# A hybrid layer on one core: seven-product pairs in every wide chunk, the plain pair first in gate/up, and four smaller moves

## The chip, the cores and the metric

One core of a Trainium2 chip runs the whole layer. The metric is device time in microseconds, from three timed runs; one further execution was profiled, and all rows come from that one. The engines are TensorE (PE, its weight loads PEld), VectorE (DVE), ScalarE (ACT), GpSimd (POOL) and SyncE (SP), which issues the loads.

## The reference, cut to what matters

256 tokens, model width 2048, all float32:

```
x = x + 0.5 * swiglu(rmsnorm(x, ffn1_norm), w_gate, w_up, w_down)       # width 5632
proj = rmsnorm(x, mix_norm) @ w_in                                      # ten parts
ro = retention(rope(rq), rope(rk), rv), normed, * silu(rg)              # 8 heads
ao = attention over the 64 best keys of each query, by an index score    # 8 heads, 2 kv
x = x + concat([ro, ao]) @ w_out                                        # 2048 x 2048
x = x + 0.5 * swiglu(rmsnorm(x, ffn2_norm), w_gate, w_up, w_down)
out = rmsnorm(x, final_norm)
```

## The kernel before, in words

**Numbers.** Every operand is split into hi and lo, both float32r: hi is ScalarE's rounding copy (line 269 for weights), lo is VectorE's difference (line 275). A product is three matmuls: hi·hi, left hi with right lo, left lo with right hi. A matmul has 512 columns.

**Wide chunks.** The gate/up, down and w_out products go in chunks of 1024 columns (`wide`, line 174): 256 tokens (two tiles, t = 0, 1) by two column halves (c = 0, 1). The contraction goes by pairs, two blocks of 128 each, 1 MB of weights a pair. A plain pair ("C") makes 8 block products of three matmuls, 24, straight into the four sums. A pair of seven products ("S", Strassen's way, Winograd's form) makes 7, so 21, in the banks of `S_BLOCKS` (line 168). For S, VectorE subtracts weight blocks from each other (line 261, four operations of 512 columns a pair), and the left side is cut into sums by `blocks_of` (line 292). A chunk's plan names its pairs: `PLAIN` has no S, `UP` is SCSCSCCC, `DOWN` has four S and then C's. The first gate/up chunk of each FFN and both w_out chunks are PLAIN; the other 20 gate/up chunks are UP; all down chunks are DOWN.

**Banks.** Eight PSUM banks. M2, M3, M4, M8 (`MAP_B`) hold the four sums 11, 12, 21, 22; M1, M5, M6, M7 hold products that several sums need (and under `MAP_A` the sums of a PLAIN chunk). After the last S pair of a chunk (`s_end`), `sums_of` (line 439) reads M1, M5, M6, M7 into the tiles u, in three steps: one copy and one addition; then the transposes of the hidden tiles of the chunk before (`turn`, line 525, in M1 and M6); then three additions. One step before the chunk's end, `ups` (line 507) adds M3 and M8 to u; at its end `hidden` (line 512) adds M2 and M4, applies silu on ScalarE and multiplies. In down and w_out, `grow` (line 457) does the like onto x.

**Order.** All is written out by hand. The list `pieces` holds the steps: a plain pair is two pieces (the first for c = 1, banks M3 and M8, the second for c = 0, M2 and M4; 12 matmuls each), an S pair four (6, 6, 6 and 3 matmuls). A load has 2048 columns, in three buffers; hi and lo have five buffers each. The loop at line 1035 goes through the pieces: in step i it runs what `after` put there, then issues the split of piece i + 4 (i + 2 for the first 11 pieces), then the matmuls of piece i:

```
        while n_split < min(n, i + ahead):
            split(n_split)
            n_split += 1
        run_step(i)
        if n_split < min(n, i + ahead + 1):
            split(n_split)
```

Each engine works its queue in that order. FFN1's chunks have numbers 0 to 5 (part 0, then down) and 6 to 10 (part 1, then down); a chunk's hidden tiles are turned in the next chunk, the left two of a chunk one for S and one plain where `DOWN` asks for it.

**Elsewhere.** `first_x`, `x_for` and `s_of_x` (lines 321 to 357) make the left sides of x from its transpose, in FFN1's first chunk as the loads come in, later from PE transposes (`turn_x`, line 359). `tables` (line 612) makes the rotation tables on VectorE, one to three operations a step, from the start of part 1 of FFN1. `first_squares` (line 655) and `rstd_tok` (line 409) give the norm. `finish` (line 571) takes squares of the last quarter of x, the norm, the products and four transfers of the output; `gain_first` (line 1025) multiplies the first half of x by the final gain, eight steps before the end.

Of the kernel before, what the change touches and what calls it, by code (L numbers as in the profile page):

```python
# [28 lines left out]
PLAIN = "CCCCCCCC"  # L29
UP = "SCSCSCCC"  # L30
# [19 lines left out]
def layer(ctx: ExitStack, tc: tile.TileContext, a: dict, out: bass.AP):  # L50
# [32 lines left out]
    MAP_A = {"11": "M7", "12": "M1", "21": "M6", "22": "M5"}  # L83
    MAP_B = {"11": "M2", "12": "M3", "21": "M4", "22": "M8"}
    turn = [0, 0]

    def pair():
        turn[0] += 1
        return [[bank["M1"], bank["M5"]], [bank["M6"], bank["M7"]]][turn[0] % 2]

    def small():
        turn[1] += 1
        return [bank["M2"], bank["M3"], bank["M4"], bank["M8"]][turn[1] % 4]
# [12 lines left out]

    now = [0]
# [66 lines left out]
    def wide(src, plan, left, cmap, x0=False):  # L174

        start = len(pieces)
        seen, last = {}, {}
        s_end = None

        def mm(i, off, a, m):  # L180

            for n, (u, v) in enumerate(((0, 0), (0, 1), (1, 0))):
                st = m not in seen
                seen[m] = 1
                e = [i, off, a, m, u, v, st, False]
                last[m] = e
                pieces[i]["mms"].append(e)

        for p, kind in enumerate(plan):
# [14 lines left out]
            if kind == "C":  # L204
                for c in (1, 0):
                    for k in range(2):
                        off = 1024 * (1 - c) + 512 * k
                        j = max(j for j, (o, n) in enumerate(tiles) if o <= off)
                        for t in range(2):
                            mm(i + j, off - tiles[j][0], (t, k), cmap[f"{t + 1}{c + 1}"])  # L210
            else:
                for k, off, a, m in S_BLOCKS:
                    mm(i + k, off, a, m)
                s_end = len(pieces)
        for e in last.values():
            e[7] = True
        return start, s_end, len(pieces) - 1, len(pieces)

    def run_mms(p, hi, lo):
        for _, off, a, m, u, v, st, sp in p["mms"]:  # L220
            TE.matmul(bank[m], lhsT=p["left"](p["pair"], a)[u], rhs=(hi, lo)[v][:, off:off + 512], start=st, stop=sp)  # L221
# [60 lines left out]
    def split_x(c, norm, xT, t=None):  # L282

        if t is None:
            t = new(one, [P, 2, 512], F32R, f"xg{c}")
# [22 lines left out]

    def s_block(pair, a):
# [99 lines left out]
    def rstd_tok(norm):  # L409
        v = new(tmp, [P, 2], F32, "sum_v", 1)  # L410
        s, k = squares[norm]
        V.tensor_reduce(v, s[:, :, :k[0]], axis=AX.X, op=OP.add)
        V.tensor_scalar(v, v, 1.0 / D, EPS, op0=OP.mult, op1=OP.add)
        r_tok[norm] = new(one, [P, 2], F32, f"r_tok{norm}")
        rsqrt(r_tok[norm], v, 2)
# [41 lines left out]
    def grow(d, scale, at, cmap, norm, done=None):  # L457
# [9 lines left out]
        def ready(c):  # L467
            for t in range(2):
                add_x(t, d, c, bank[cmap[f"{t + 1}{c + 1}"]], scale)

        if s_end is not None:
            after(s_end, early)
        after(half, lambda: ready(1))
# [9 lines left out]
    marks = {}  # L483

    def ffn(which, norm, next_norm, last):
        wgu, wd = a[f"wgu{which}"], [a[f"wd{which}{j}"] for j in range(2)]
        c = 0
        for part, n in enumerate(PARTS):
            hs = {}
            marks[which, part] = len(pieces)  # L490
            for cc in range(n):
                cmap = MAP_A if c == 0 else MAP_B
# [4 lines left out]
                if s_end is not None:  # L497
                    after(s_end, lambda u=u: sums_of(u))

                def full(b, u=u, cmap=cmap):  # L500

                    if b in u:
                        tt(u[b], u[b], bank[cmap[b]])
                        return u[b]
                    return bank[cmap[b]]

                def ups(u=u, full=full):
                    for b in ("12", "22"):
                        if b in u:
                            full(b)  # L510

                def hidden(u=u, full=full, cc=cc, part=part, hs=hs, cmap=cmap):
                    ht, sil = [], []
                    for t in range(2):
                        g = full(f"{t + 1}1")
                        s = u[f"{t + 1}1"] if u else new(tmp, [P, W], F32, "s")
                        S.activation(s, g, AF.Silu, scale=r_tok[norm][:, t:t + 1])  # L517
                        sil.append(s)
                    for t in range(2):
                        b = f"{t + 1}2"  # L520
                        ht.append(u[b] if u else new(tmp, [P, W], F32, "e", 3))
                        V.scalar_tensor_tensor(ht[t], u[b] if u else bank[cmap[b]], r_tok[norm][:, t:t + 1], sil[t],  # L522
                                               op0=OP.mult, op1=OP.mult)

                    def turn(m, q):
# [5 lines left out]
                        if DOWN[part][k] == "S":  # L531
                            f = half_k("b")
                            S.activation(f, v, AF.Copy)
                            hs[k] = blocks_of(f, big(F32R, (P, 4, 2, P)), big(F32R, (P, 3, 2, P)))
                        else:
                            h = big(F32R, (P, 2, 512))
                            S.activation(h[:, :, :T], v, AF.Copy)
                            V.tensor_tensor(h[:, :, T:], v, h[:, :, :T].bitcast(F32), op=OP.subtract)
                            hs[k] = h
# [8 lines left out]
            for d in range(2):  # L548
                at = wide(wd[part][d], DOWN[part], left_of(hs), MAP_B)
                start, s_end, half, end = at  # L550
                final = last and part == 1 and d == 1
                if part == 1 and d == 0:
                    after(end, lambda: act_table(AF.Sqrt))
                grow(d, 0.5, at, MAP_B, next_norm if part == 1 and not final else None)
                if final:
                    after(end, finish)
                elif part == 1 and not last:
                    if d == 0:
                        turns = list(range(4))
                    else:  # L560
                        for i, m in enumerate(("M1", "M5", "M6", "M7")):
                            after(s_end + 2 + i, lambda i=i, m=m: turn_x(i, next_norm, m))
                        turn_rest(end, next_norm)
        return end

    def turn_rest(end, norm):

        for s, c, m in ((0, 6, "M3"), (0, 7, "M8"), (1, 4, "M2"), (1, 5, "M4")):
            after(end + s, lambda c=c, m=m: turn_x(c, norm, m))

    def finish():

        for c in (1, 0):
            for t in range(2):
                square_x(3, t, halves(2 + c).start, 512)
        rstd_tok(3)
        for t in range(2):
            r = r_tok[3][:, t:t + 1]
            xs = [x[t][:, halves(c, 1024)] for c in range(2)]
            S.activation(xs[0], xs[0], AF.Copy, scale=r)  # L580
            V.scalar_tensor_tensor(xs[1], xs[1], r, last_gain[1], op0=OP.mult, op1=OP.mult)
            for c in range(2):
                nc.sync.dma_start(out[t][:, halves(c, 1024)], xs[c])
# [20 lines left out]
    V.memset(ones, 1.0)  # L604
    act_table(AF.Copy)
# [6 lines left out]
    def tables(at_sin):  # L612
# [13 lines left out]
        yield 1  # L626
        V.tensor_scalar(n, n, MAGIC, None, op0=OP.add)
        yield 1
        V.tensor_scalar(n, n, MAGIC, None, op0=OP.subtract)
        for c in (C1, C2, C3):  # L630
            yield 1
# [3 lines left out]
        yield 1  # L635

        V.tensor_scalar(n, ang, 1.0 / C_TWO_PI, MAGIC, op0=OP.mult, op1=OP.add)
        yield 1
        V.tensor_scalar(n, n, MAGIC, None, op0=OP.subtract)
        for c in (C1, C2, C3):  # L640
            yield 1
            V.scalar_tensor_tensor(ang, n, -c, ang, op0=OP.mult, op1=OP.add)
        yield 1
        V.tensor_scalar(ang, ang, PI_DOWN, -PI_DOWN, op0=OP.min, op1=OP.max)
        yield 1
# [208 lines left out]
    def attend(pair):  # L854
# [17 lines left out]
        m = big(F32R, (P, 2, 512))  # L872
# [260 lines left out]
```

## Time and profile before

| what | value |
|---|---|
| three timed runs | 1887.64, 1888.31, 1888.44 us; median 1888.31 |
| the profiled execution | 1887.65 us |
| its span, first to last instruction | 1885.8 us |
| TensorE, VectorE, ScalarE busy | 98%, 86%, 56% |
| matmuls | 8624 |
| weights and other reads | 355.76 MB, 190 GB/s over the span |
| chain that ended last, by engine | PE 93%, DVE 5%, ACT 1%, issue 1% |
| granted TensorE clock, mean | 0.997 |

The chain is followed back from the last instruction: at each step to what released it. A row of the timeline gives start, duration, engine, line, operation, what is written and read, how many alike were merged, and in brackets the idle time before it with what ended it. Matmuls overlap in it: each has its full passage as duration, and the next starts before it ends.

### The profile page before, as it was taken

How to read it: one execution, taken by the hardware profiler on the slowest of the kernel's cores; microseconds unless marked ns; L12 is line 12 of the kernel's file. 1: busy time of each engine (PE TensorE's matmuls, PEld its weight loads, DVE VectorE, ACT ScalarE, POOL GpSimd, SP SyncE). 2: the span in 40 equal slices, each digit the busy share in tenths (PEclk: the TensorE clock that was granted, in tenths of full speed). 3: DMA queues.
4: the chain of work that ended last, by engine and by line, in shares of the span. 5: the costliest groups of instructions: out<-in, count | busy, mean ns of one | idle time of the engine just before them, and what ended most of it. 6: DMA issues, size and time to landing. Idle time of an engine off the chain costs nothing.

```text
span 1885.8 us, 22691 instructions
## 1 busy us (share of the span) xinstructions
PE 1856.2 (98%) x8624; PEld 1527.1 (81%) x8624; DVE 1625.8 (86%) x2076; ACT 1064.9 (56%) x1348; POOL 5.3 (0%) x14
## 2 busy tenths in 40 slices
PE   8999999999999999999999999999999999999997
PEld 6788888887888887988888888788888888888886
DVE  7899998889999997789865756799999889999997
ACT  7555655544555555656544555555555455555554
POOL 0000000000000000000000000000000000000000
PEclk9999999999999999999999999999999999999998
DMA  8544555545555454545534444545555555455454
GB/s 323 191 178 180 199 201 221 192 170 178 194 206 203 172 208 156 187 164 211 179 134 173 168 174 178 198 181 191 209 203 180 199 201 200 180 191 210 180 198 159
DMA packets 51309, 359.33 MB, mean 191 GB/s; under 512 B 5856, under 2 KB 5856, under 8 KB 8704
## 3 DMA queue, kind: packets, MB, share of 16 engines
q1 hardware_dynamic: 50400, 355.62, 51.6%
q8 instruction: 67, 1.10, 0.2%
q10 hardware_dynamic: 432, 1.08, 0.2%
q0 software_dynamic: 368, 1.19, 0.2%
q14 instruction: 42, 0.34, 0.1%
HBM read 355.76 MB, written 2.10 MB: 190 GB/s over the span
## 4 chain that ended last, share of the span: by engine, by line
PE 93%; DVE 5%; ACT 1%; issue 1%; DMA 0%; DVEq 0%; ACTq 0%
PE M L221 75%; PE M L145 8%; PE M L147 4%; DVE lo L275 2%; PE M L529 1%; PE M L163 1%; PE M L164 1%; PE M L162 1%; DVE raw L261 1%; DVE x L434 1%; ACT hi L269 1%; PE M L790 0%; DVE e L437 0%; PE M L838 0%; PE M L144 0%
## 5 line engine op out<-in xcount | busy, mean ns | idle before, releaser
L269 ACT ACTIVATE hi<-raw 128x1024 fp32r<-128x1024 f32 (+2 forms) x853 | 843.9, 1008 | 578.8 <-DVE raw L261 356.3
L275 DVE TENSOR_TENSOR lo<-raw,hi 128x1024 fp32r<-128x1024 f32 (+2 forms) x853 | 974.5, 1160 | 152.7 <-ACT hi L269 137.7
L221 PE MATMUL M<-hi,xg 128*128 128x512 f32 x2240 | 738.3, 396 | 1.4 <-DVE e L437 1.4
L221 PE MATMUL M<-hi,mid 128*128 128x512 f32 x1696 | 531.1, 392 | 8.2 <-ACT hi L269 7.8
L221 PEld LDWEIGHTS M<-hi,xg 128*128 128x128 f32 x2240 | 422.6, 189 | 99.5 <-DVE e L437 1.9
L221 PE MATMUL M<-lo,xg 128*128 128x512 f32 x1120 | 444.4, 397 | 2.3 <-DVE lo L275 2.1
L221 PEld LDWEIGHTS M<-hi,mid 128*128 128x128 f32 x1696 | 319.4, 188 | 75.9 <-ACT hi L269 7.8
L221 PE MATMUL M<-lo,mid 128*128 128x512 f32 x848 | 331.5, 391 | 0.1
L261 DVE TENSOR_TENSOR raw<-raw 128x512 f32<-128x512 f32 x368 | 254.7, 692 | 12.4
L221 PEld LDWEIGHTS M<-lo,xg 128*128 128x128 f32 x1120 | 211.4, 189 | 56.7 <-DVE lo L275 8.7
L145 PE MATMUL M<-xg,hi 128*128 128x512 f32 x688 | 245.2, 398 | 1.3 <-DVE xg L289 1.1
L221 PEld LDWEIGHTS M<-lo,mid 128*128 128x128 f32 x848 | 159.8, 188 | 34.6 <-DVE lo L275 1.8
L147 PE MATMUL M<-xg,lo 128*128 128x256 f32 x645 | 182.1, 282 | 0.0
L145 PEld LDWEIGHTS M<-xg,hi 128*128 128x128 f32 x688 | 128.3, 188 | 30.7 <-DVE xg L289 2.2
L221 PE MATMUL M<-hi,ext 128*128 128x512 f32 x360 | 142.4, 395 | 1.9 <-DVE e L522 1.7
L147 PEld LDWEIGHTS M<-xg,lo 128*128 128x128 f32 x645 | 121.4, 188 | 0.8
L221 PEld LDWEIGHTS M<-hi,ext 128*128 128x128 f32 x360 | 67.8, 188 | 18.9 <-DVE e L522 2.6
L221 PE MATMUL M<-lo,ext 128*128 128x512 f32 x180 | 71.2, 395 | 0.1
L437 DVE TENSOR_TENSOR s<-s,M 128x512 f32<-128x512 f32 x96 | 64.1, 682 | 2.2 <-PE M L221 1.2
L517 ACT ACTIVATE s<-s,r_tok 128x512 f32<-128x512 f32 x40 | 27.0, 718 | 54.6 <-DVE s L437 54.6
L221 PEld LDWEIGHTS M<-lo,ext 128*128 128x128 f32 x180 | 33.9, 188 | 8.3 <-DVE lo L275 0.5
L704 ACT ACTIVATE b<-e 64x512 f32<-64x512 f32 (+2 forms) x46 | 28.1, 612 | 19.5 <-DVE e L690 18.9
(173 smaller groups left out, 910.2 us busy)
## 6 DMA issues: line engine op xcount, KB each, us to landing
raw<-in_wgu SPq DMA_DIRECT2D x175, 1024.0 KB, 4.8
raw<-in_wd SPq DMA_DIRECT2D x88, 1024.0 KB, 4.8
raw<-in_w_out SPq DMA_DIRECT2D x16, 1024.0 KB, 4.8
raw<-in_w_iq SPq DMA_DIRECT2D x8, 1024.0 KB, 4.8
raw<-in_w_aq SPq DMA_DIRECT2D x8, 1024.0 KB, 4.8
raw<-in_w_rk SPq DMA_DIRECT2D x8, 1024.0 KB, 4.9
raw<-in_w_rq SPq DMA_DIRECT2D x8, 1024.0 KB, 4.8
raw<-in_w_rv SPq DMA_DIRECT2D x8, 1024.0 KB, 4.8
```

Of the source, the lines that this page charges most:

```text
L145: TE.matmul(acc, lhsT=hi[:, c:c + P], rhs=r, start=st, stop=sp)
L147: TE.matmul(acc[:, T:], lhsT=lo[:, c:c + P], rhs=r[:, :T], start=False, stop=False)
L162: TE.matmul(o, lhsT=h, rhs=hi[:, i * n:(i + 1) * n], start=st, stop=False)
L163: TE.matmul(o, lhsT=h, rhs=lo[:, i * n:(i + 1) * n], start=False, stop=False)
L164: TE.matmul(o, lhsT=l, rhs=hi[:, i * n:(i + 1) * n], start=False, stop=sp)
L221: TE.matmul(bank[m], lhsT=p["left"](p["pair"], a)[u], rhs=(hi, lo)[v][:, off:off + 512], start=st, stop=sp)
L261: V.tensor_tensor(r[:, o:o + 512], r[:, a:a + 512], r[:, b:b + 512], op=OP.subtract)
L269: S.activation(hi[:, :p["n"]], raw, AF.Copy)
L275: V.tensor_tensor(lo[:, :p["n"]], raw, hi[:, :p["n"]].bitcast(F32), op=OP.subtract)
L437: V.tensor_tensor(o, a, b, op=OP.add)
L517: S.activation(s, g, AF.Silu, scale=r_tok[norm][:, t:t + 1])
L704: S.activation(b[p0:p0 + w], q[p1:p1 + w], AF.Copy)
```

## The change

All gate/up chunks take a new plan CSCSCSCC, both w_out chunks SCSCSCCC. `PLAIN`, `MAP_A` and the plain copies of x for S pairs are gone. 14 matmuls of a tile of ones are issued ahead of everything else. `tables` goes on every third step instead of every step. In the last down chunk the last two pairs' products of token tile 0 come first and those of tile 1 are put behind them all, and `finish` ends tile by tile. `gain_first` moves from eight to three steps before the end. Lines that are left out only follow renamed arguments or reshape the weights to the new plans.

```
-PLAIN = "CCCCCCCC"
-UP = "SCSCSCCC"
+UP = "CSCSCSCC"
+OUT = "SCSCSCCC"
 DOWN = ("SCSCSCSCCCCC", "SCSCSCSCCC")
...
-    MAP_A = {"11": "M7", "12": "M1", "21": "M6", "22": "M5"}
-    MAP_B = {"11": "M2", "12": "M3", "21": "M4", "22": "M8"}
+    SUM = {"11": "M2", "12": "M3", "21": "M4", "22": "M8"}
...
-    def wide(src, plan, left, cmap, x0=False):
+    def wide(src, plan, left, x0=False, tail=False):
...
                         for t in range(2):
-                            mm(i + j, off - tiles[j][0], (t, k), cmap[f"{t + 1}{c + 1}"])
+                            if tail and p >= len(plan) - 2:
+                                ending[t].append((i + j, off - tiles[j][0], p, (t, k), SUM[f"{t + 1}{c + 1}"]))
+                                continue
+                            mm(i + j, off - tiles[j][0], (t, k), SUM[f"{t + 1}{c + 1}"])
...
+        ending[1].sort(key=lambda e: e[4], reverse=True)
+        for t in range(2):
+            for i, off, p, a, m in ending[t]:
+                mm(i, off, a, m, i if t == 0 else len(pieces) - 1)
...
+    def left_pair(kind, v, in_psum=True):
+
+        if kind == "S":
+            if in_psum:
+                f = half_k("b")
+                S.activation(f, v, AF.Copy)
+                v = f
+            return blocks_of(v, big(F32R, (P, 4, 2, P)), big(F32R, (P, 3, 2, P)))
+        t = big(F32R, (P, 2, 512))
+        S.activation(t[:, :, :T], v, AF.Copy)
+        V.tensor_tensor(t[:, :, T:], v, t[:, :, :T].bitcast(F32), op=OP.subtract)
+        return t
...
         if UP[c] == "S":
-            split_x(c, norm, xT, big(F32R, (P, 2, 512)))
             s_of_x(c, norm, xT)
...
+        if final:
+            after(end, lambda: finish(ready))
+            return
         after(half, lambda: ready(1))
         after(end, lambda: ready(0))
...
-                start, s_end, half, end = wide(wgu[c], PLAIN if c == 0 else UP, left_of(xg if c == 0 else xs), cmap,
-                                               c == 0 and which == 1)
+                start, s_end, half, end = wide(wgu[c], UP, left_of(xs), c == 0 and which == 1)
...
+                def ups(u=u):
                     for b in ("12", "22"):
-                        if b in u:
-                            full(b)
+                        tt(u[b], u[b], bank[SUM[b]])
+
+                def hidden(u=u, cc=cc, part=part, hs=hs):
+                    for b in ("11", "21"):
+                        t = int(b[0]) - 1
+                        tt(u[b], u[b], bank[SUM[b]])
+                        S.activation(u[b], u[b], AF.Silu, scale=r_tok[norm][:, t:t + 1])
...
+    def turn_early(s_end, norm):
+
+        for i, m in enumerate(("M1", "M5", "M6", "M7")):
+            after(s_end + 2 + i, lambda i=i, m=m: turn_x(i, norm, m))
+
+    def turn_late(end, norm, banks):
+
+        for i, s in ((2, 0), (3, 0), (0, 1), (1, 1)):
+            after(end + s, lambda i=i: turn_x(4 + i, norm, banks[i]))
+
+    def finish(ready):
+
+        for t in range(2):
+            r = None
+            for c in (1, 0):
+                ready(c, (t,))
                 square_x(3, t, halves(2 + c).start, 512)
+            rstd_tok(3, slice(t, t + 1))
             r = r_tok[3][:, t:t + 1]
+            for c in range(4):
+                xs = x[t][:, halves(c)]
+                if c < 2:
+                    S.activation(xs, xs, AF.Copy, scale=r)
+                else:
+                    V.scalar_tensor_tensor(xs, xs, r, last_gain[1][:, halves(c - 2)], op0=OP.mult, op1=OP.mult)
+                nc.sync.dma_start(out[t][:, halves(c)], xs)
...
+    for _ in range(14):
+        TE.matmul(bank["M1"][:, :P], lhsT=ones, rhs=ones, start=True, stop=True)
     act_table(AF.Copy)
...
-        yield 1
+        yield 3
         V.tensor_scalar(n, ang, 1.0 / C_TWO_PI, None, op0=OP.mult)
-        yield 1
+        yield 3
...
-        m = big(F32R, (P, 2, 512))
-        v = ps.rearrange("p (j q) -> p j q", j=2)
...
+        mix[4 + pair] = left_pair(OUT[pair], ps.rearrange("p (j q) -> p j q", j=2))
...
+        mix[c] = left_pair(OUT[4 + c], f, False)
...
     for d in range(2):
-        cmap = (MAP_A, MAP_B)[d]
-        at = wide(a["w_out"][d], PLAIN, left_of(mix_in), cmap)
-        grow(d, 1.0, at, cmap, 2)
+        at = wide(a["w_out"][d], OUT, left_of(mix_in))
+        grow(d, 1.0, at, 2)
         if d == 0:
             after(at[3], lambda: act_table(AF.Sqrt))
-            for i, m in enumerate(("M1", "M5", "M7", "M6")):
-                c = (2, 3, 0, 1)[i]
-                after(at[3] + 3 + 2 * i, lambda c=c, m=m: turn_x(c, 2, m))
-    turn_rest(at[3], 2)
+    turn_early(at[1], 2)
+    turn_late(at[3], 2, ("M6", "M7", "M1", "M5"))
...
-    after(end - 8, gain_first)
+    after(end - 3, gain_first)
```

## Rows read from the trace of the kernel before

**Rows 1.** The page's first part: busy us, share of the span, instructions.

```profile
PE 1856.2 (98%) x8624; PEld 1527.1 (81%) x8624; DVE 1625.8 (86%) x2076; ACT 1064.9 (56%) x1348; POOL 5.3 (0%) x14
```

**Rows 2.** Windows by stage: stretch, length, then each engine's busy us, clock, DMA.

```profile
85.48:129.09 43.61, 43.61 (x192) 35.24 (x192) 41.58 (x52) 25.22 (x31) 0.00 (x0) 1.00 0.53 194
...
415.00:454.48 39.48, 35.58 (x141) 26.95 (x139) 38.83 (x48) 16.58 (x19) 0.00 (x0) 0.96 0.50 177
...
721.60:758.00 36.40, 32.69 (x177) 26.42 (x177) 26.65 (x46) 20.33 (x40) 0.00 (x0) 1.00 0.34 124
758.00:1071.00 313.00, 313.00 (x1828) 273.20 (x1828) 231.00 (x357) 176.51 (x264) 3.34 (x6) 1.00 0.48 173
1071.00:1160.00 89.00, 89.00 (x403) 73.57 (x403) 54.20 (x67) 45.96 (x64) 0.00 (x0) 1.00 0.54 189
```

**Rows 3.** The chain in order of time: start, length, what (two long pieces).

```profile
85.48 42.73 PE M L221 x183
...
1076.90 46.30 PE M L221 x204
```

**Rows 4.** Timeline of VectorE around the end of gate/up chunk 2.

```profile
127.00 0.68 DVE L437 TENSOR_TENSOR s<-s,M 128x512 f32<-128x512 f32 x1
...
129.32 0.29 DVE L296 TENSOR_TENSOR sq<-b 128x128 f32<-128x128 f32 x1 [0.36 <-ACT b L533]
...
131.04 0.69 DVE L306 TENSOR_TENSOR mid<-sq,mid 128x512 fp32r<-128x512 f32 x1 [0.16 <-ACT mid L302]
...
135.66 1.22 DVE L275 TENSOR_TENSOR lo<-raw,hi 128x1024 fp32r<-128x1024 f32 x1
136.91 2.15 DVE L261 TENSOR_TENSOR raw<-raw 128x512 f32<-128x512 f32 x3
138.97 1.22 DVE L275 TENSOR_TENSOR lo<-raw,hi 128x1024 fp32r<-128x1024 f32 x1
...
141.97 1.28 DVE L437 TENSOR_TENSOR e<-e,M 128x512 f32<-128x512 f32 x2
...
143.77 1.28 DVE L437 TENSOR_TENSOR s<-s,M 128x512 f32<-128x512 f32 x2
```

**Rows 5.** Timeline of FFN1's first chunk: its start, and the second chunk's first matmul.

```profile
8.67 1.06 ACT L269 ACTIVATE hi<-raw 128x1024 fp32r<-128x1024 f32 x1 [0.35 <-DMA raw<-in_wgu]
...
9.24 1.05 PE L221 MATMUL M<-hi,mid 128*128 128x512 f32 x2
...
13.61 0.62 PE L221 MATMUL M<-hi,mid 128*128 128x512 f32 x2
...
55.76 0.50 PE L221 MATMUL M<-hi,ext 128*128 128x512 f32 x1 [0.86 <-DVE e L522]
```

**Rows 6.** Timeline of TensorE around the same chunk end: the transposes, the next chunk's first.

```profile
128.05 1.03 PE L529 MATMUL M<-ident,e 128*128 128x128 f32 x8
...
142.86 0.39 PE L221 MATMUL M<-hi,ext 128*128 128x512 f32 x1
```

**Rows 7.** Groups of VectorE by line: count, busy us, mean ns, idle before.

```profile
L289 DVE SCALAR_TENSOR_TENSOR xg<-M,gains,xg 128x256 fp32r<-128x256 f32 x26 | 12.2, 481 | 8.5 <-ACT xg L288 8.5
...
L632 DVE SCALAR_TENSOR_TENSOR mid<-mid,mid 128x1024 f32<-128x1024 f32 x3 | 3.7, 1218 | 0.0
```

**Rows 8.** Timeline of the end, and the output tile's transfers.

```profile
1873.19 1.37 DVE L434 SCALAR_TENSOR_TENSOR x<-M,x 128x512 f32<-128x512 f32 x2 [1.35 <-PE M L221]
...
1873.44 0.39 PE L221 MATMUL M<-hi,mid 128*128 128x512 f32 x1
...
1876.83 2.48 DVE L581 SCALAR_TENSOR_TENSOR x<-x,r_tok,mid 128x1024 f32<-128x1024 f32 x2
...
DMA to landing us min/median/max: 2.6/3.9/4.8
```

**Rows 9.** Timeline of TensorE: two stops in the stretch of the tables.

```profile
428.67 0.50 PE L221 MATMUL M<-lo,xg 128*128 128x512 f32 x1 [1.82 <-DVE lo L275]
...
449.11 0.50 PE L221 MATMUL M<-hi,xg 128*128 128x512 f32 x1 [1.43 <-DVE e L437]
```

More of the change, by code (lines that the diff above doesn't have):

```diff
@@ L184, in mm @@
                 seen[m] = 1
[L185 removed]
+                e = [i, off, (pieces[i]["pair"], a), m, u, v, st, False]
                 last[m] = e
[L187 removed]
+                pieces[i if at is None else at]["mms"].append(e)
         for p, kind in enumerate(plan):
@@ L217, in wide, with run_mms @@
         return start, s_end, len(pieces) - 1, len(pieces)
-    def run_mms(p, hi, lo):
-        for _, off, a, m, u, v, st, sp in p["mms"]:
-            TE.matmul(bank[m], lhsT=p["left"](p["pair"], a)[u], rhs=(hi, lo)[v][:, off:off + 512], start=st, stop=sp)
+    def run_mms(p):
+        for i, off, (pair, a), m, u, v, st, sp in p["mms"]:
+            TE.matmul(bank[m], lhsT=p["left"](pair, a)[u], rhs=split_of[i][v][:, off:off + 512], start=st, stop=sp)
     def block(src, l0, l1, width):
@@ L280, in gain, with split_x @@
         return gains[:, norm * KT + 2 * c + j:norm * KT + 2 * c + j + 1]
-    def split_x(c, norm, xT, t=None):
-        if t is None:
-            t = new(one, [P, 2, 512], F32R, f"xg{c}")
+    def split_x(c, norm, xT):
+        t = new(one, [P, 2, 512], F32R, f"xg{c}")
         for j in range(2):
@@ L407, in row_of, with rstd_tok @@
         return ps[:, :T]
-    def rstd_tok(norm):
-        v = new(tmp, [P, 2], F32, "sum_v", 1)
+    def rstd_tok(norm, ts=slice(0, 2)):
+        v = new(tmp, [P, 2], F32, "sum_v", 1)[:, ts]
         s, k = squares[norm]
-        V.tensor_reduce(v, s[:, :, :k[0]], axis=AX.X, op=OP.add)
+        V.tensor_reduce(v, s[:, ts, :k[ts.start]], axis=AX.X, op=OP.add)
         V.tensor_scalar(v, v, 1.0 / D, EPS, op0=OP.mult, op1=OP.add)
-        r_tok[norm] = new(one, [P, 2], F32, f"r_tok{norm}")
-        rsqrt(r_tok[norm], v, 2)
+        if norm not in r_tok:
+            r_tok[norm] = new(one, [P, 2], F32, f"r_tok{norm}")
+        rsqrt(r_tok[norm][:, ts], v, ts.stop - ts.start)
     def rstd(norm):
@@ L548, in ffn @@
             for d in range(2):
-                at = wide(wd[part][d], DOWN[part], left_of(hs), MAP_B)
+                final = last and part == 1 and d == 1
+                at = wide(wd[part][d], DOWN[part], left_of(hs), tail=final)
                 start, s_end, half, end = at
-                final = last and part == 1 and d == 1
                 if part == 1 and d == 0:
                     after(end, lambda: act_table(AF.Sqrt))
-                grow(d, 0.5, at, MAP_B, next_norm if part == 1 and not final else None)
+                grow(d, 0.5, at, next_norm if part == 1 else None, final)
@@ L571, in finish @@
-    def finish():
-        for c in (1, 0):
-            for t in range(2):
+                    pass
+                elif part == 1 and not last and d == 1:
+                    turn_early(s_end, next_norm)
+                    turn_late(end, next_norm, ("M2", "M4", "M3", "M8"))
+        return end
+    def turn_early(s_end, norm):
[4 more added lines that the diff above has]
+            after(end + s, lambda i=i: turn_x(4 + i, norm, banks[i]))
```

99 lines of the change are left out of this document (26 added, 73 removed).

## The prediction, made before the result was known

> **What bounds the kernel now.** I read the engine totals first: TensorE is busy 98% of the span, VectorE 86% [rows 1]. An average hides which stage is tight, so I then read the windows by stage [rows 2]. In a settled gate/up chunk (85.48 to 129.09) TensorE is busy all 43.61 us and VectorE 41.58 us, 95%. In w_out (1071 to 1160) VectorE has 54.20 of 89 us to do, in the mixing stage 231 of 313. So TensorE sets the pace, and in gate/up VectorE is almost the bound as well. The chain gives the pace [rows 3]: 42.73/183 = 0.233 us a matmul with x on the left, 46.30/204 = 0.227 with hidden or mix tiles. Last I read VectorE's queue around one chunk's end [rows 4]: it runs in the order of the program, and from 127.00 to 145.05 its longest pause is 0.36 us. That order decides my forecast.
>
> I add to the profiled execution, 1887.65 us (span 1885.8), which lies 0.66 us under the median of the three runs. A measurement of this kernel can tell about 0.2%, 3.8 us, from no change.
>
> **Part 1: 36 matmuls fewer.** A plain pair issues 24 matmuls, a seven-product pair (S) 21. New are 3 S pairs in the first chunk of each FFN and 3 in each w_out chunk, 12 in all. FFN2's 9 matmuls give 9 x 0.233 = 2.1, w_out's 18 give 18 x 0.227 = 4.1: **-6.2**. FFN1's 9 are in part 4. FFN2's first chunk also loses the wait at its end, whose twin in FFN1 stands at 55.76 with 0.86 of idle [rows 5]: **-1.0**, with the slower matmul behind it. The loads stay 1 MB a pair, on the same queue, and ScalarE (56% busy, [rows 1]) has room for four copies more per new S pair: 0, and at most the 2 us that each pair's copies last if it had none.
>
> **Part 2: the chunk's end in gate/up.** The ring of pairs stays the same (three plain ones behind the last S), but the boundary moves: S C S C S C C C becomes C S C S C S C C, so two plain pairs, not three, lie between the last S and the chunk's end. VectorE's queue from there on is now: sums, split, turn, split, three additions, S0, S1, S2, `ups`, S3, `hidden` (S0 to S3 are the splits of the next S pair). The first additions of `hidden` free M2 and M4. After the change it is: sums, split, turn, split, three additions, S0, `ups`, S1, `hidden`, S2, S3. S1, with three subtractions and one lo, stands ahead of `hidden`, since a split is issued four pieces ahead: it is piece end+3, issued in step end-1.
>
> The walk: the transposes start at 128.05 [rows 6], so the last S ended at 128.05 - 12 x 0.2325 = 125.26. Up to the three additions and S0 (135.66 to 136.88) nothing changes [rows 4]. Then `ups` takes 1.28, to 138.1 (M3 free at 137.5). S1 lasts from 136.91 to 140.19 now, 3.3, so it ends at 141.4, and the first addition of `hidden` frees M2 at 142.0. TensorE would pass the chunk's end at 125.26 + 0.87 (transposes) + 4 x 2.79 = 137.29. It waits 0.2 for M3, runs the plain pair's first piece (M3, M8) to 140.3, and then waits for M2 until 142.0: 1.75. Together 1.95. Behind that matmul stand only others of TensorE; ScalarE's next hi copies wait for the buffers they free, VectorE for neither. Today the chunk ends at 142.86 [rows 6], M2 is asked for 2.1 later and free at 144.45 [rows 4]: it fits by 0.5. The change takes 5.6 us of TensorE's work out of this stretch, 2.6 (S2, S3) of VectorE's, and asks 0.7 later: 0.5 - 3.0 + 0.7 = -1.8, the same answer.
>
> This holds where a turned tile is cut for S (129.32 to 131.73, 2.4 us of VectorE, [rows 4]): at the ends of chunks 1 to 4 and 7 to 9 of each FFN, 14 places: 14 x 1.95 = **+27.3**. Chunks 0 and 6 turn nothing and are 3 us ahead: no wait. The other bound is 0, were VectorE further ahead at the last S than today; its splits there wait for buffers that TensorE frees, so I don't expect it.
>
> From gate/up to down, 4 places: down begins with S, so M3 is asked for 0.7 and M2 2.0 us behind the end, and S1 is split even ahead of the three additions. By the same walk: 0.4 + 0.6 + 0.8 (the next lo) = 1.8 with two plain tiles turned (chunk 5), 2.1 + 0.5 + 0.5 = 3.1 with an S tile (chunk 10). 2 x 1.8 + 2 x 3.1 = **+9.8**, between 3 and 13.
>
> **Part 3: w_out and its end.** Each chunk gains 3 x 4.5 us of VectorE (four subtractions of 0.7, 1.7 more of lo) and 5.5 of sums and additions: 19 on 27, for 41.5 of TensorE. It just fits; the boundary between the two chunks I put at 0.5. The end is worse: x0 to x3 are now turned behind the second chunk's last S, two of them cut for S, x4 to x7 at its end, one for S, and S1 is split ahead of the last two additions. The nearest row is FFN1's end, turned in the same steps with plain tiles only: 36.40 - 32.69 = 3.7 us of idle [rows 2]. Three S tiles cost 2.4 - 0.96 more each [rows 4, 7], 4.4 in all, and S1 2.1: 10.2. Part lies beside the plain pair between, so I take 8, bounds 0 (as today) and 13: **+8.5** with the boundary. The S cut of two attention pairs and one retention pair (1.7 each) lies in the mixing stage under TensorE, with 82 us of VectorE free [rows 2]: 0; without that cover 5.
>
> **Part 4: the start.** FFN1's first chunk becomes VectorE's. A plain pair costs it 0.96 for x [rows 7] and 2.4 for lo, 3.4; an S pair 2.4 + 2.8 + 4.1 = 9.3, against 4.8 of TensorE. The third tile of weights is there for 8.67, so its lo starts at 9.8 [rows 5]. From there 1.2 + 3 x 9.3 + 4 x 3.4 + 1.4 (rstd) = 44 us: the last S lo at 47, the lo behind it at 49.2. Four plain pieces follow, 11.1 us: chunk 1 starts at 60, against 55.76 now. **+4**, between -6 (TensorE alone the bound) and +7. The 14 idle matmuls run while TensorE waits for weights, and cost nothing. They can lift the clock: at 9.24 two matmuls take 1.05 us, at full pace 0.62 [rows 5], so some ten run 0.2 too long, 2.0 in all. In my walk VectorE ends the chunk, and nothing comes of it.
>
> The Trainium skill, page "TensorE: Matmul & The Clock Gate", section "What's actually happening", says that the throttled state is the default and that activity releases it. By that rule alone the start would be 2 us shorter and the sum 1923; the trace agrees that TensorE begins at the low level, and the sum here makes no use of it.
>
> **Part 5: tables.** From 415 to 454.48 TensorE idles 39.48 - 35.58 = 3.9 us, and 0.04 x 39.48 = 1.6 of clock is lost [rows 2]: 5.5. The same 14 us of VectorE's work (six of 1.22 [rows 7], the rest shorter) now go over 50 pieces, two chunks with 2 us of room each, but three pieces of 1.22 fall in front of `hidden` at two ends: 3.5 left. **-2.0**, between -5.5 and +2. Its one transfer is issued in the same step as before.
>
> **Part 6: the end.** The last two additions begin at 1873.19, rstd is there at 1876.83, the products last until 1879.3, the last of four transfers lands up to 4.8 behind its issue, near 1884.5, and the span ends at 1885.8, 12.0 behind the last matmul [rows 8]. After: token tile 0 is done 24 matmuls (5.4 us) ahead and leaves under them. For tile 1: addition 0.7, square 0.8, rstd 1.4, its four quarters by 4.5, issue 0.4, landing 2.6 (the least of now), 1.3: 8.6 with the moved `gain_first` (2.4) just ahead of tile 0's additions, which costs 0.3. **-3.4**, between -2.3 and -4.3.
>
> **Sum:** -6.2 - 1.0 + 27.3 + 9.8 + 8.5 + 4.0 - 2.0 - 3.4 = +37.0: 1924.65, so 1925.
>
> **Rivals.** (a) **Faster:** VectorE is in time at the chunk ends and in w_out. Then parts 2 and 3 cost nothing and all of part 5 comes back: -6.2 - 1.0 + 4.0 - 5.5 - 3.4 = -12: 1875.5. For it: VectorE is busy 86% only. Against: its queue has no gap there. It decides where M2 is free less than 14.8 us behind the last S; I have 16.7. Chance 0.16. (b) **Half the waits:** 1 us at each of 14 ends, 9 at w_out and down together, -8.6 + 23: 1902. Chance 0.18. (c) **The clock falls too:** TensorE idled 1.82 us before 428.67 and ran seven matmuls 0.2 too long behind it, while 1.43 us of idle before 449.11 did nothing of the kind [rows 9]; my wait is 1.6 by that count. If all 18 bring it, 18 x 1.4 = 25: 1950. Chance 0.12. (d) Gains and waits cancel: 0.04.
>
> **How the numbers follow.** The forecast has 0.50, its own range 1908 to 1939. With (b), (d) and most of (c) the range is 1885 to 1948. Faster 0.16, within 0.2% 0.04, slower 0.80.
>
> **What would show it.** Right: waits of TensorE of 1 to 2 us for the addition (line 437's, from `hidden`) at 14 chunk ends, and a settled period near 45.5 us; longer ones where FFN2 begins; chunk 1 starting near 60; the span's end 8 to 9 us behind the last matmul. Wrong: a settled period of 43.4 or less, or chunk 1 starting before 55.

## The result: slower, 1933.67 us against 1888.38

The changed kernel takes 1933.67 us (median of six runs, 1932.73 to 1934.51), the kernel before 1888.38 (six runs, 1887.36 to 1888.65): a ratio of 1.0241, 95% interval 1.0227 to 1.0254. The profiled execution took 1932.88 us, its span is 1931.1, 45.3 longer than before. The forecast was 1925, between 1885 and 1948.

### The profile page after: what moved, and what is told of

It reads as the page before. It is cut to its first block, busy times and chain, and to the rows that moved or that the text cites. A ratio compares the mean times of both kernels' runs of the same rounds, so it can differ in the third digit from the quotient of the medians.

```text
span 1931.1 us, 22887 instructions
## 1 busy us (share of the span) xinstructions
PE 1867.9 (97%) x8616; PEld 1524.3 (79%) x8616; DVE 1694.4 (88%) x2194; ACT 1090.1 (56%) x1375; POOL 5.3 (0%) x14
## 4 chain that ended last, share of the span: by engine, by line
PE 74%; DVE 19%; ACT 3%; issue 2%; DMA 1%; SPq 0%; DVEq 0%; ACTq 0%
PE M L229 58%; DVE lo L283 7%; PE M L144 7%; DVE raw L269 4%; PE M L146 4%; DVE e L457 2%; ACT hi L277 2%; DVE s L457 1%; DVE x L454 1%; PE M L162 1%; PE M L161 1%; PE M L163 1%; PE M L536 1%; DMA raw<-in_wgu 1%; ACT sq L394 1%
## 5 line engine op out<-in xcount | busy, mean ns | idle before, releaser
L277 ACT ACTIVATE hi<-raw 128x1024 fp32r<-128x1024 f32 (+1 forms) x877 | 870.1, 1005 | 604.2 <-DVE raw L269 399.4
L283 DVE TENSOR_TENSOR lo<-raw,hi 128x1024 fp32r<-128x1024 f32 (+1 forms) x877 | 998.5, 1155 | 143.9 <-ACT hi L277 132.9
L229 PE MATMUL M<-hi,xg 128*128 128x512 f32 x2288 | 765.5, 398 | 27.1 <-DVE s L457 20.2
L229 PE MATMUL M<-hi,mid 128*128 128x512 f32 x1588 | 498.8, 392 | 6.4 <-DVE e L457 3.5
L229 PEld LDWEIGHTS M<-hi,mid 128*128 128x128 f32 x1588 | 299.0, 188 | 74.3 <-DVE e L457 5.4
L229 PE MATMUL M<-lo,mid 128*128 128x512 f32 x794 | 310.5, 391 | 1.0 <-DVE lo L283 1.0
L269 DVE TENSOR_TENSOR raw<-raw 128x512 f32<-128x512 f32 x416 | 287.5, 691 | 12.3
L229 PEld LDWEIGHTS M<-lo,mid 128*128 128x128 f32 x794 | 149.4, 188 | 33.2 <-DVE lo L283 3.1
L229 PE MATMUL M<-hi,ext 128*128 128x512 f32 x396 | 156.6, 396 | 0.0
L457 DVE TENSOR_TENSOR e<-s,M 128x512 f32<-128x512 f32 x64 | 43.7, 683 | 1.1
```

The source lines that it names most:

```text
L229: TE.matmul(bank[m], lhsT=p["left"](pair, a)[u], rhs=split_of[i][v][:, off:off + 512], start=st, stop=sp)
L269: V.tensor_tensor(r[:, o:o + 512], r[:, a:a + 512], r[:, b:b + 512], op=OP.subtract)
L277: S.activation(hi[:, :p["n"]], raw, AF.Copy)
L283: V.tensor_tensor(lo[:, :p["n"]], raw, hi[:, :p["n"]].bitcast(F32), op=OP.subtract)
L457: V.tensor_tensor(o, a, b, op=OP.add)
```

## The profile after

The page's first part and the chain's shares by engine. They answer to [rows 1] and to the small table:

```profile
PE 1867.9 (97%) x8616; PEld 1524.3 (79%) x8616; DVE 1694.4 (88%) x2194; ACT 1090.1 (56%) x1375; POOL 5.3 (0%) x14
...
PE 74%; DVE 19%; ACT 3%; issue 2%; DMA 1%; SPq 0%; DVEq 0%; ACTq 0%
```

TensorE has 36 matmuls of the layer fewer and is nevertheless busy 11.7 us longer, 5.8 of them with the idle ones. VectorE is busy 68.6 us longer, and its share of the chain has gone from 5% to 19%. The list of waits, in us in total, times, longest, says for what TensorE waits; before, the largest entries of its wide matmuls were 7.8 (one wait, the start) and 2.1:

```profile
PE M L229 <- DVE s L457: 20.2, 16, 1.4
...
PE M L229 <- DVE lo L283: 7.3, 13, 1.0
...
PE M L383 <- DVE x L454: 5.2, 7, 2.4
PE M L229 <- DVE e L457: 4.9, 3, 1.8
PE M L229 <- ACT hi L277: 3.7, 3, 1.7
```

The first entry is the addition of `hidden` that the forecast named: 14 times about 1.35 us, and twice 0.6, behind chunks 0 and 6 of FFN1, where the forecast had no wait. Windows by stage, with the columns of [rows 2]: FFN1's first chunk, a settled gate/up chunk (M2's wait to M2's wait), the two w_out chunks, the first 55 us of FFN2.

```profile
6.59:62.00 55.41, 47.73 (x186) 34.48 (x185) 50.21 (x80) 39.44 (x67) 0.00 (x0) 0.97 0.73 282
65.78:111.19 45.41, 43.93 (x191) 35.11 (x192) 41.67 (x53) 25.66 (x31) 0.00 (x0) 1.00 0.50 185
...
1091.78:1184.80 93.02, 88.11 (x396) 70.96 (x394) 84.21 (x110) 54.20 (x74) 0.00 (x0) 1.00 0.52 192
1184.80:1240.00 55.20, 50.09 (x206) 39.74 (x205) 48.13 (x71) 32.12 (x47) 0.00 (x0) 0.94 0.41 152
```

A settled chunk has the same matmuls and the same 41.6 us of VectorE as before, but takes 45.41 us where [rows 2] have 43.61: 1.80 more without any more work. Where it goes, the two timelines of such a chunk's end show, VectorE's first, then TensorE's:

```profile
104.85 1.22 DVE L283 TENSOR_TENSOR lo<-raw,hi 128x1024 fp32r<-128x1024 f32 x1
105.98 1.28 DVE L457 TENSOR_TENSOR e<-e,M 128x512 f32<-128x512 f32 x2
107.18 2.14 DVE L269 TENSOR_TENSOR raw<-raw 128x512 f32<-128x512 f32 x3
109.23 1.22 DVE L283 TENSOR_TENSOR lo<-raw,hi 128x1024 fp32r<-128x1024 f32 x1
110.37 1.28 DVE L457 TENSOR_TENSOR s<-s,M 128x512 f32<-128x512 f32 x2
```

```profile
106.29 0.99 PE L229 MATMUL M<-hi,xg 128*128 128x512 f32 x2
...
109.45 0.39 PE L229 MATMUL M<-hi,xg 128*128 128x512 f32 x1
111.19 0.47 PE L229 MATMUL M<-hi,xg 128*128 128x512 f32 x1 [1.35 <-DVE s L457]
```

This is the order that the prediction walked through: S0, `ups`, S1 (three subtractions and a lo, 107.18 to 110.45), `hidden`. Its first addition begins at 110.37 and takes about 0.7, and the matmul that needs M2 starts at 111.19, 1.74 behind the last one where 0.23 is usual. The first matmul on M3, the second of the two at 106.29, starts 0.52 behind the one before it, 0.29 late; together that makes the 1.80.

Table: the difference of the two profiled executions by stretch, each from its first matmul to the next one's, in us. A settled end counts 1.80.

| stretch | before | after | of it settled ends | rest | forecast of the rest |
|---|---|---|---|---|---|
| start to the first down chunk (FFN1) | 273.82 | 288.12 | 4 x 1.80 | +7.1 | +4.0 |
| gate/up part 1 with the tables | 224.05 | 226.74 | 3 x 1.80 | -2.7 | -2.0 |
| w_out and FFN2's gate/up part 0 | 354.58 | 370.67 | 4 x 1.80 | +8.9 | +1.3 (-7.2 + 8.5) |
| FFN2's gate/up part 1 | 216.82 | 222.35 | 3 x 1.80 | +0.1 | 0 |
| the four down stretches | 468.87 | 477.91 | 0 | +9.0 | +9.8 |
| mixing | 335.69 | 335.33 | 0 | -0.4 | 0 |
| behind the last matmul | 12.01 | 9.97 | 0 | -2.0 | -3.4 |

The 14 settled ends make 25.2 (forecast 27.3), the rest 20.0 (forecast 9.7): 45.2 against 37.0.

## The experiments

Run 1 is experiment 1, and so on. Each kernel is compared with the changed one, 1933.67, unless another is named. Times stand for one run each, except in experiment 5; the kernel before took 1887.0 to 1889.0 beside them. Six runs of the changed kernel lie 1.8 us apart, so less than 2 us between two single runs says nothing by itself; there the stretches of the table are compared. Where the code is the same, these agree within 0.6 us between the traces (the last down stretch: 108.85, in run 6 108.30), except for FFN1's start: runs 3, 6 and 9, which share it with the changed kernel, reach the first down chunk at 288.24, 288.81 and 289.27, the changed kernel at 288.12.

**1. The order of VectorE's queue at the chunk's end.** The split that stands ahead of `hidden` is issued behind it, at the borders between two gate/up chunks alone.

```
+    hold = set()
...
+                if cc < n - 1:
+                    hold.add(end)
...
-        while n_split < min(n, i + ahead):
+        while n_split < min(n, i + ahead - (i in hold)):
...
-        if n_split < min(n, i + ahead + 1):
+        while n_split < min(n, i + ahead + 1 - (i + 1 in hold)):
```

> The changed kernel with one edit: where a gate/up chunk follows a gate/up chunk, the split that is three pieces ahead of the boundary's end (the second piece of the next S pair, three subtractions and a lo, 3.3 us of VectorE) is issued behind the additions that free M2 and M4, not ahead of them. No work is added or taken away. My theory (the order of VectorE's queue makes the wait): the wait of 1.5 us for M2 at 14 chunk ends falls below 0.5, the settled period goes from 45.40 to 43.5 to 44.0, the two shorter waits behind chunks 0 and 6 go too, and the time is 1911, give or take 4. Rival (VectorE has simply too much to do, 95% of its time): the wait only moves to the next S pair, the period stays above 45 and the time above 1928.

Measured: 1910.96, so 22.7 less. VectorE around the same chunk end, then TensorE:

```profile
104.03 1.22 DVE L284 TENSOR_TENSOR lo<-raw,hi 128x1024 fp32r<-128x1024 f32 x1
105.17 1.28 DVE L458 TENSOR_TENSOR e<-e,M 128x512 f32<-128x512 f32 x2
106.36 1.28 DVE L458 TENSOR_TENSOR s<-s,M 128x512 f32<-128x512 f32 x2
```

```profile
105.47 1.00 PE L230 MATMUL M<-hi,xg 128*128 128x512 f32 x2
106.31 0.39 PE L230 MATMUL M<-lo,xg 128*128 128x512 f32 x1
```

The additions of `hidden` now come 1.2 us behind `ups` and not 4.4, and no stop is left but the 0.3 for M3 (two matmuls in 1.00 us for 0.62): a settled chunk takes 43.82 us. The same work, one place later in one queue: the wait was one of order, not of VectorE's load, as the theory had it.

**2. The old order in the new kernel.**

```
-UP = "CSCSCSCC"
+UP = "SCSCSCCC"
```

> The changed kernel with the gate/up plan back at SCSCSCCC, now in all 22 chunks, so the number of S pairs is that of the changed kernel and only the place of the boundary is that of before. My theory: settled period 43.6, the 14 waits gone (25 us), the four gate/up-to-down ends back to about 0.5 (7 us), FFN1's start later by 1 to 5 us since the first pair is now cut for S: 1903, give or take 6. Rival (the added S pairs cost the time, not the order): at least 1920.

Measured: 1910.78, between the two forecasts and 1.8 above the first one's range. The 14 waits and those around the down chunks are gone (the four down stretches as before), but FFN1 now reaches its first down chunk at 285.38, later than before by 11.6, and from the start of w_out to the end of FFN2's part 0 it takes 370.25 us, no less than with the plain pair first. A first chunk of seven-product pairs is dear in either order. The plain pair first makes FFN1's start cheaper: 7.1 there instead of 11.6.

**3. w_out plain again.** The first reading of the 16 us that w_out and FFN2's start lose was that the pairs of seven in w_out fill VectorE.

```
-OUT = "SCSCSCCC"
+OUT = "CCCCCCCC"
...
-        ps = small() if c < 3 else bank["M8"]
+        ps = small() if c < 3 else bank["M1"]
...
-    turn_early(at[1], 2)
+    turn_early(at[3] - 6, 2)
```

> The changed kernel with plain pairs in w_out (18 matmuls more, 4.1 us; the last retention tile in M1 instead of M8), and x turned in the same four steps ahead of the chunk's end and at it. My theory: w_out and FFN2's first chunk together lose 13 us more to waits than w_out's saved matmuls give; without the additions and subtractions of S in w_out's end VectorE is ahead by 10 us there, so these two stages shorten by some 9 and the time is 1925, give or take 4. Rival (the waits come from cutting x for S in FFN2's first chunk, whatever w_out does): the 18 matmuls come on top, 1937.

Measured: 1931.92, 1.75 less, between the two. That theory fell: VectorE has 34 us less to do in the stretch from w_out to the end of FFN2's part 0 (experiment 7 shows it), and the stretch is 1.3 us shorter.

**4. Without the idle matmuls.** The 14 matmuls of ones are left out.

> The changed kernel without the 14 matmuls of ones at its beginning. My theory (VectorE ends FFN1's first chunk): the first matmuls run at the lower clock, yet chunk 1 starts within 1 us of where it starts now, and the time is within 1.5 us of the changed kernel's. Rival (TensorE's clock sets the start): 2 us or more later.

Measured: 1933.72, as expected. Chunk 1 begins at 61.96 (in the changed kernel 62.20) and the first down chunk at 288.68, inside the scatter of this start, so the idle matmuls have no effect that these runs can show. In the trace after, they fill 1.06 to 6.8 (28 records for 14), and two matmuls at 7.42 take 0.62 us, where [rows 5] have 1.05; but the splits are late all the same:

```profile
1.06 5.78 PE L609 MATMUL M<-ones 128*128 128x128 f32 x28 [1.06 <-DVE ones L607]
6.59 0.48 PE L229 MATMUL M<-hi,xg 128*128 128x512 f32 x1
...
7.42 0.62 PE L229 MATMUL M<-hi,xg 128*128 128x512 f32 x2
...
10.54 0.51 PE L229 MATMUL M<-lo,xg 128*128 128x512 f32 x1 [0.42 <-DVE lo L283]
14.35 0.50 PE L229 MATMUL M<-lo,ext 128*128 128x512 f32 x1 [0.75 <-DVE lo L283]
```

Without them the same two matmuls take as long as in the kernel before:

```profile
7.41 1.05 PE L229 MATMUL M<-hi,xg 128*128 128x512 f32 x2
```

**5. The small parts alone.** The kernel before with the tables on every third step, the last chunk and `finish` by token tile, the later `gain_first`, and the idle matmuls; no new plan.

> The kernel before with four parts of the change and none of its plans: the rotation tables on every third step, the last down chunk and finish by token tile with the first half's gain three steps before the end, and the 14 matmuls of ones ahead of all. Theory (each part is worth here what the trace after showed of it: tables 2.7 us less by the stretch of part 1, tail 2.0 less, idle matmuls 0.5 less): 1888.4 - 5.2 = 1883.2, between 1881.5 and 1885; faster than before and than any kernel so far. Rival (the tables' gain in the changed kernel only gave back waits that the new order had brought, and the tail's moved the waiting forward): 1886 or more.

Measured over eleven runs: 1883.87 (1882.23 to 1884.45) against 1887.35 (fifteen runs), ratio 0.9979, interval 0.9970 to 0.9988: 0.2% faster than the kernel before, a small difference but clear of the noise, and as expected. The windows of the gate/up part with the tables and of the time behind the last matmul, before and then in this kernel:

```profile
399.89:623.94 224.05, 220.15 (x949) 175.91 (x947) 214.34 (x270) 123.15 (x143) 0.00 (x0) 0.99 0.51 188
1873.83:1885.84 12.01, 0.00 (x1) 0.00 (x0) 4.19 (x10) 3.79 (x7) 0.00 (x0) 0.61 0.44 175
```

```profile
399.90:622.22 222.32, 218.74 (x948) 176.48 (x947) 213.42 (x270) 122.93 (x143) 0.00 (x0) 0.99 0.51 189
1872.23:1882.17 9.94, 0.01 (x1) 0.00 (x0) 3.85 (x11) 3.08 (x8) 0.00 (x0) 0.69 0.58 211
```

So -1.7 and -2.1; the first down chunk begins at 273.87 in place of 273.82, so the idle matmuls bring nothing here.

**6. The squares later.** In the trace after, four of the eight squares of x's last half run on ScalarE from 1199.07 to 1201.5, ahead of three hi copies, and TensorE waits 1.72 us for the first of these.

```
-            after(end + 2, squares_)
+            after(end + (8 if norm == 2 and d == 1 else 2), squares_)
...
-    after(at[3] + 5, lambda: rstd_tok(2))
+    after(at[3] + 11, lambda: rstd_tok(2))
```

> The changed kernel with ScalarE's eight squares of the last half of x, and the norm behind them, six steps later in FFN2's first chunk. Theory (the squares at 1199.2 to 1201.6 stand ahead of the rounding copies for which TensorE waits 1.72 and 0.76 us behind 1202.6, and the idle time lowers the granted clock at 1204.2 for 3.4 us): the two waits and the slow stretch go, 2.5 + 1.7 = 4.2 less: about 1929.5. Rival (VectorE's cutting of x for the three pairs of seven sets the pace there, and the squares only hide beside it): within 1 us of the changed kernel, 1932.5 or more.

Measured: 1932.41, 1.3 less, which lies within the scatter; from w_out's start to the end of FFN2's part 0 it takes 369.87 us, 0.8 less than after. That is all but the rival's forecast (1932.5 or more) and far from the theory's 1929.5. ScalarE and TensorE there:

```profile
1211.12 0.61 ACT L394 ACTIVATE sq<-x 128x512 f32<-128x512 f32 x1
...
1211.73 2.94 ACT L277 ACTIVATE hi<-raw 128x1024 fp32r<-128x1024 f32 x3
```

```profile
1202.37 0.50 PE L229 MATMUL M<-lo,xg 128*128 128x512 f32 x1 [0.18 <-DVE lo L283]
...
1214.09 0.51 PE L229 MATMUL M<-lo,xg 128*128 128x512 f32 x1 [0.76 <-DVE lo L283]
1239.92 0.48 PE L229 MATMUL M<-hi,xg 128*128 128x512 f32 x1 [1.10 <-DVE s L457]
```

The wait at 1202 is down to 0.18, but the three hi copies are late ten us further on, and the end of the chunk, which had no wait there after, now has one of 1.10. The squares only pass the lateness on, and the theory fell; that VectorE sets the pace there instead, as the rival has it, is not shown by this run.

**7. The order alone.** The kernel before with nothing but `UP` changed to CSCSCSCC; first chunks and w_out stay plain.

> The kernel before with the plan of its twenty gate/up chunks of seven-product pairs changed from SCSCSCCC to CSCSCSCC and nothing else: first chunks and w_out stay plain. Theory (the order by itself brings the waits of 1.8 us for the additions at the ends of gate/up chunks and those of 2 us at the down chunks, as the changed kernel shows): by the segments that changed, 4 ends x 1.8 in each part 0, 4.2 and 5.3 in the two parts 1, and 9.0 around the down chunks: 14.4 + 9.5 + 9.0 = 33, so 1921, between 1916 and 1925. Rival (the pairs of seven in the first chunks and in w_out, with the late work that they leave, carry most of the loss): 1905 or less.

Measured: 1919.97, 32.6 above the kernel before: as expected. It has the 14 ends (TensorE waits 1.37 us for the addition at 147.60, the period is 45.40) and the late borders of the down chunks. The order is the larger part of the loss; the rest is in the first chunks and w_out. For w_out and FFN2's part 0 as one stretch, the windows of four kernels stand side by side: before, with the order alone, after, and with plain w_out (run 3):

```profile
1070.81:1425.39 354.58, 353.72 (x1568) 288.04 (x1567) 289.86 (x363) 196.82 (x250) 0.00 (x0) 1.00 0.51 187
```

```profile
1087.32:1448.06 360.74, 354.66 (x1568) 287.65 (x1567) 287.20 (x359) 198.96 (x250) 0.00 (x0) 1.00 0.50 184
```

```profile
1091.78:1462.45 370.67, 354.73 (x1541) 284.36 (x1540) 336.15 (x430) 213.15 (x267) 0.00 (x0) 0.99 0.50 182
```

```profile
1091.81:1461.19 369.38, 357.41 (x1559) 287.27 (x1558) 302.47 (x379) 202.15 (x251) 0.00 (x0) 0.99 0.49 180
```

The order costs 6.2 here, FFN2's first chunk of seven-product pairs with its turned x 8.6 (369.38 - 360.74), and w_out's own pairs 1.3, although they bring most of VectorE's extra work. The same subtraction at FFN1's start gives 288.68 - 279.21 = 9.5 for its first chunk (run 4 less this one, both without idle matmuls); the table has 7.1, since with the order alone chunk 1 starts at 54.08, 1.7 earlier than before. The spread tables give 4.2 in the new order (this run's part 1 takes 230.93, after 226.74), the end 2.0; 0.6 is between run 4's start and that of the changed kernel, within its scatter. So 32.6 + 9.5 + 8.6 + 1.3 - 4.2 - 2.0 - 0.6 = 45.2. Each part is the difference of a stretch between two kernels that differ in it, so the parts have to add up; that they do is no proof of its own, and those of FFN1's start are good to about 1 us.

**8. The borders of the down chunks.** Run 1 with the late split also there.

```
-                if cc < n - 1:
-                    hold.add(end)
+                hold.add(end)
+                if cc == n - 1:
+                    hold.add(half)
...
+                hold.add(end)
+                if d == 0:
+                    hold.add(half)
```

> The kernel with the late split, with the same done at the borders of the down chunks: the pieces of the next chunk's first pair of seven that VectorE cut ahead of the additions there are cut behind them (at a gate/up or down chunk that a seven-product pair follows, its third and fourth piece; at a down chunk that a plain pair follows, the second piece of the pair behind it). Theory (the 9.0 us that the four down stretches lost against before, with the waits of 1.8 us behind 642.8 and 0.3 behind 293.7 in the trace after, are the same fault, additions queued behind cuts of weights): at least half of it comes back, 4 to 9 less than the 1910.96 of the late split, so 1902 to 1907. Rival (VectorE is a full 1 to 2 us late at these borders whatever its order is, since the last two of the chunk before are plain pairs only and not three): the waits pass from the additions to the lo copies, 1909.5 or more.

Measured: 1909.07, 1.9 less than run 1: nearer to the rival. The four down stretches together take 476.6 us, after 477.8 in run 1, so 1.2 of it is theirs; the first of them is 1.1 longer. TensorE at the border into FFN1's second down part:

```profile
635.25 0.51 PE L230 MATMUL M<-hi,mid 128*128 128x512 f32 x1 [1.27 <-DVE s L458]
638.06 0.50 PE L230 MATMUL M<-lo,mid 128*128 128x512 f32 x1 [0.25 <-DVE lo L284]
639.35 0.50 PE L230 MATMUL M<-lo,mid 128*128 128x512 f32 x1 [0.32 <-DVE lo L284]
```

After, one wait of 1.77 for `ups` stood there (before 644.98). Now it is 1.27 for `hidden`, 0.25 and 0.32 for the lo copies: VectorE is late at these borders in either order. In run 2, where three plain pairs and not two lie behind the chunk's last pair of seven, the four stretches are as before.

**9. x0 to x3 turned earlier.** Run 3 with the turns where the kernel before has them. In the kernel before they stand in the second w_out chunk from its third step; the change puts them behind that chunk's last pair of seven, since until then its products hold the banks.

```
-    turn_early(at[3] - 6, 2)
+            for i, m in enumerate(("M1", "M5", "M7", "M6")):
+                c = (2, 3, 0, 1)[i]
+                after(at[3] + 3 + 2 * i, lambda c=c, m=m: turn_x(c, 2, m))
```

> The changed kernel with plain w_out chunks, as in the run of that name, and with x0 to x3 turned and cut where the kernel before does it, from the third step of the second w_out chunk, not behind its seventh pair. Theory A (the lateness at the start of FFN2 comes from the place: cutting x0 to x3 stands between the additions and splits at the end of w_out, and a plain w_out leaves the banks free to do it 11 us and more earlier): most of the 8.6 us by which w_out and FFN2's first stretch there exceed those of the kernel with the order alone come back: 1923 to 1927 against 1931.92. Theory B (FFN2's first chunk is late because it is one of seven-product pairs: eight subtractions and cuts of its own weights more, and three x tiles cut for them): within 2 us of 1931.92.

Measured: 1927.44, just over theory A's range. The same stretch:

```profile
1092.73:1457.10 364.37, 355.74 (x1560) 286.47 (x1559) 302.31 (x379) 201.88 (x251) 0.00 (x0) 1.00 0.50 182
```

5.0 of the 8.6 come back with the place alone, with as much work on VectorE. The other 3.6 stay. TensorE's idle of 1.85 and 0.76 us before 1196.85 and 1198.11, for hi and lo copies that come behind four squares, is of that size, but run 6 shows that moving the squares alone hardly helps. So both theories hold a part, A the larger.

## Why the prediction was right, and where it was not

**Part 2, the ends in gate/up: right.** Forecast 1.95 at 14 ends by a walk through VectorE's queue (0.2 for M3, 1.75 for M2), measured 1.80 at as many (0.29 and 1.51). Run 1 undoes the order and 22.7 us come back; run 7 does the order alone and 32.6 appear, with the down borders in them. The pair that the prediction named, S1 ahead of `hidden`, is the cause shown.

**The borders of down: right in size.** 9.8 forecast, 9.0 measured: 1.4 at each part 0 and 2.9 and 3.3 at the parts 1, for 1.8 and 3.1. Its mechanism is only partly that of the 14 ends: run 8 moves the splits and gets 1.2 back in these stretches, run 2 with three plain pairs behind the last S all of it.

**Part 3 is the step that failed.** "I take 8, bounds 0 and 13", with 7.2 saved in matmuls and a wait: +1.3 in all, measured +8.9. With the 7.2 counted as saved, waits and clock took 16.1, above the bound of 13. Of the 8.9, 6.3 lie in FFN2's first chunk (52.61 us to the next chunk's first matmul, before 46.31) and 2.4 in the second w_out chunk. The prediction saw the late turning of x0 to x3 and priced it too low, from FFN1's end with S cuts on top: its place alone costs 5.0 (run 9). What it did not see was (i) the squares ahead of the hi copies in ScalarE's queue, though without them there only 0.8 comes back (run 6); (ii) 1.67 us at w_out's start, where a matmul at 1099.59 waits until the last retention tile has left M8; (iii) the clock: behind the idle of 2.35 us before 1190.17 and 1.72 before 1202.61 it was granted at 0.50, 1.2 GHz, in two stretches. By an estimate, half of each stretch, that is up to 1.7 in each. What makes up the other 3.6 of the 8.6 that FFN2's first chunk lost stays open.

```profile
1202.61 0.50 PE L229 MATMUL M<-hi,xg 128*128 128x512 f32 x1 [1.72 <-ACT hi L277]
```

```profile
1190.52:1193.93 3.41, 3.16 (x11) 0.50 0.00 0
1204.17:1207.58 3.41, 3.41 (x9) 0.50 0.44 132
```

(columns: TensorE alone, then clock and DMA). "It just fits" does not follow from the prediction's own numbers: 27 and 19 are 46 us of VectorE for 41.5 of TensorE. That w_out fitted all the same was luck: measured, VectorE was busy 84.21 of the two chunks' 93.02 us, and run 3 puts w_out's own pairs at 1.3.

**Part 4: the start.** Forecast +4.0, measured +7.1. Chunk 1 was to start at 60 and starts at 62.2 (before 55.76), and the end of chunk 0, for which no wait was foreseen, has one of 0.62 us. The walk took VectorE to be busy without a break, and the last S pair's lo copies ready at 47. They are ready at 48.42: from 9.3 to there VectorE itself pauses ten times for 0.15 us or more, 2.9 us in all, for ScalarE. The longest pause, and those lo copies:

```profile
37.56 0.29 DVE L303 TENSOR_TENSOR sq<-b 128x128 f32<-128x128 f32 x1 [0.61 <-ACT b L344]
...
46.60 1.82 DVE L283 TENSOR_TENSOR lo<-raw,hi 128x1024 fp32r<-128x1024 f32 x2
```

The walk also left out the four sums of the chunk itself, 4 x 0.69 us of VectorE from 54.52. They stand ahead of the addition for which TensorE waits the 0.62; no run sets their share apart. That the 14 idle matmuls would cost nothing and bring nothing held: no effect beyond the scatter in run 4, none in run 5. The two matmuls at 7.42 ran at full pace behind them, 0.62 us, and at 1.05 without them (run 4). The rule of the Trainium skill that the prediction quotes (page "TensorE: Matmul & The Clock Gate", section "What's actually happening") is that activity releases the throttle; these rows agree with it. The 2 us that this was to give are hidden, since TensorE then waits for the lo copies.

**Part 5: right** in sign and near in size: -2.7 for -2.0. Alone it is worth 1.7 in the old order (run 5), in the new one 4.2 (run 7 against the changed kernel), so its worth hangs on the order.

**Part 6: too hopeful**, -2.0 for -3.4. The rows of the end:

```profile
1920.74 0.39 PE L229 MATMUL M<-hi,mid 128*128 128x512 f32 x1
...
1921.34 1.28 DVE L454 SCALAR_TENSOR_TENSOR x<-M,x 128x512 f32<-128x512 f32 x2
1922.12 0.63 ACT L394 ACTIVATE sq<-x 128x512 f32<-128x512 f32 x1 [0.78 <-DVE x L454]
...
1924.88 1.41 DVE L585 SCALAR_TENSOR_TENSOR x<-x,r_tok,mid 128x512 f32<-128x512 f32 x2
```

```profile
L586 SPq DMA_DIRECT2D out_T<-x x8: 332/373/458, 1920.8 to 1927.2; - x8
...
DMA to landing us min/median/max: 2.2/2.6/2.9
```

Two squares follow the additions, not one, so the last product is there at 1926.3, 5.2 behind the last matmul and not 4.5; and the last of eight issues starts at 1927.2, 0.9 behind it and not 0.4. The prediction's own terms also add up to 8.8, not 8.6. Tile 1 has all of this behind the last matmul; 2.6 to landing and 1.3 to the span's end are as reckoned.

**The rivals.** (a) and (b) needed VectorE to be in time; run 1 shows that it could have been, with another order. (c), the clock falling at all 18 places, did not come: the settled window above has clock 1.00 with 1.35 us of idle at its end, and of the four borders of down one was followed by 0.50, the last.

## What to carry to other kernels

Where VectorE is 95% busy under a bound TensorE, the order of its queue is a resource of its own: before moving a boundary, write down which evacuation frees which bank and which prefetch work stands ahead of it, and issue the prefetch behind it. Work that a plan saves on the bound engine is worth nothing at a boundary where the helper is late; small edits elsewhere (run 5) brought the 3.5 us that twelve cheaper pairs did not. When several parts go into one change, run each alone: here those with a gain of 3.5 us were hidden behind a loss of some 49.

## What the runs showed of the hardware that was not expected

The idle time ahead of a matmul did not alone decide on the clock: in the changed kernel it stayed at 1.00 behind 1.77 us (644.98) and 1.87 (495.99), and fell to 0.50 behind 1.72 (1202.61, with another stop of 0.76 right after) and 1.77 (1814.91). In FFN1's first chunk the same two stops, 1.62 and 0.94 us, were followed by 0.50 in the changed kernel (from 47.05) and by 1.00 in runs 6, 8 and 9. A float32 matmul of ones, 14 in the program, left 28 records in the trace. And a stop can be missing from the idle times: the 0.29 at M3 stands in none, since the matmul before it, 0.39 long, had not ended for part of it, and the rest is too short for the list.
